# The first 24 units of a hybrid encoder layer: written order, split square sums, and a shorter dt product

## The chip, the cores and the metric

The kernel runs on one core of a Trainium2 chip. The time is device microseconds of that core for one execution. TensorE (PE; its weight loads are listed as PEld) multiplies, VectorE (DVE), ScalarE (ACT) and GpSimd (POOL) do the elementwise work, and loads are issued on the queues of SyncE (SP) and GpSimd. Products go to PSUM, from which the other engines collect them.

## The reference

The kernel computes one step of a two-layer encoder trunk on 256 prompt tokens and 64 sample tokens, 320 columns in all, with a model width of 2048. Each layer modulates a normalized input with a shift and a scale that depend on a condition vector, mixes, normalizes and adds:

```python
def modulate(x, c, w_ada, b_ada, g_pre):
    mod = jax.nn.silu(c) @ w_ada + b_ada
    shift, scale, gate = jnp.split(mod[:, None, :], 3, axis=-1)
    return rms_norm(x, g_pre) * (1 + scale) + shift, gate

# the even layer: state space heads and sliding-window attention share one input projection
z, xbc, dt_raw, q, k, v, g_att = jnp.split(h @ w_in, cuts, axis=-1)
xbc, conv_new = causal_conv(xbc, conv_prev, conv_w)
dt = jax.nn.softplus(dt_raw + dt_bias)
# ... chunked scan, attention with sinks, gates, norm ...
out = jnp.concatenate([y_ssm, y_att], axis=-1) @ w_out
```

The odd layer is a gated short convolution between two projections. All inputs and outputs are 32-bit.

## The kernel before

Features lie on the 128 partitions, tokens along the free dimension. A k-tile is 128 input features, 16 of them for the width 2048. A unit is 128 output features of a projection: 16 k-tiles, each with three products of 128x128 weights and 128x320 activations. Both operands are split into a rounded part and a rest (`wh` and `wl` of the weights, `hh` and `hl` of the activations), and the products are wh.hh, wh.hl and wl.hh (L169 to L171 in `block`). `split` makes wh on ScalarE (L149) and wl on VectorE (L150), eight weight tiles at a time.

The first layer begins while nothing is known. The input x (four tiles of four k-tiles) is squared on ScalarE and summed on VectorE in two chains over all 16 k-tiles (`sumsq`, L325 and L329); three small products, `ss0t`, sum over the partitions; `rstd` refines an inverse root on VectorE from a bit trick in three rounds and spreads it to all partitions with the products `r0b`. Meanwhile the modulation (shift and scale, one pair of numbers per feature) comes from products with `w_ada`: the first k-tile's from the first half of a small table (`ada_first`, tiles `adaf`), the second's from its other half, those of the others by blocks of 512 columns (two k-tiles, 4 MB each) in four loads of 1 MB and 16 products each (`ada_pe`, L219, tiles `adap`). The last block of the scale and shift, block 7, is multiplied on VectorE instead (`ada_side`, L250, tiles `adas` and `adac`), at a rate of 0.24 k-tiles per four entries of a product block. `modulate` makes hh and hl of a k-tile: a step on VectorE (L341), hh on ScalarE (L342), hl on VectorE (L343), each for the prompt and the sample columns apart.

Since the modulation arrives slowly, the first 24 units (k, v, and two of the four query and gate groups) go through the k-tiles in pieces: k-tile 0 for all 24 units, k-tile 1 for all, then k-tiles 2 and 3, 4 to 7, 8 to 11 and 12 to 15. After each piece the result of a unit is added from PSUM into a tile in memory (`start_unit`, L416; the first piece is copied by ScalarE, L405). The tiles of k, v, q and g are `acc`, `q` and `g`.

A scheduler sets the order of each engine's instructions, by priorities, and moves independent ones past each other; the order in the source is a start. Buffers: weights `w` in 3 buffers of 1 MB (the loads of `ada_pe` use them too), large activations in 21 buffers G, small ones in 20 buffers S, PSUM in 3 + 4 + 1 banks.

After the 24 units come attention, the other projections of the even layer with the scan, its output projection, and the odd layer. `dt` is one unit of 32 useful columns (48 products, tile `pdt`) behind the query and gate units.

Of the kernel before, what the change touches and what calls it, by code (L numbers as in the profile page):

```python
# [8 lines left out]
F32 = mybir.dt.float32  # L9
F32R = mybir.dt.float32r  # L10
# [14 lines left out]
SPE = 20  # L25
WAIT_S, WAIT_T = 6, 2
AHEAD = 3
RATE_0, RATE_A, RATE_B, RATE_C, RATE_D = 0.24, 0.55, 0.2, 0.6, 0.14
# [4 lines left out]
def hybrid_stream_step(ctx: ExitStack, tc: tile.TileContext, i, o):  # L33
    nc = tc.nc
    V, S, G, PE = nc.vector, nc.scalar, nc.gpsimd, nc.tensor
# [40 lines left out]
    for g in range(4):  # L76
        nc.sync.dma_start(xin[g], i["xT"][:, 4 * g : 4 * g + 4, :])
# [4 lines left out]
    for n in range(2):  # L82
        nc.sync.dma_start(early[n][:, 0:8, :], i["ws1"][0][n])
# [17 lines left out]
    S.activation(cs[:, :, 0:2], cT, AF.Silu)  # L101
    es = const.tile([128, 2, 32], F32, name="es")
# [5 lines left out]
    jobs, tasks, wait = [], [], [0]  # L108
# [39 lines left out]
    def split(dst_h, dst_l, src):  # L148
        S.activation(dst_h, src, AF.Copy)  # L149
        V.tensor_tensor(dst_l, src, dst_h.bitcast(F32), op=ALU.subtract)  # L150

    def block(src, name, entries, h, pool=wp):


        if early:
            w = early.pop(0)
        else:
            w = pool.tile([128, 16 if pool is wp else 8, 128], F32, tag="w" if pool is wp else "G", name=name)
            nc.sync.dma_start(w[:, 0 : len(entries), :], src)
        for hf in range(len(entries) // 8):  # L160
            wh = wp.tile([128, 8, 128], F32R, tag="wh", name=f"{name}h{hf}")
            wl = wp.tile([128, 8, 128], F32R, tag="wl", name=f"{name}l{hf}")
            split(wh, wl, w[:, 8 * hf : 8 * hf + 8, :])

            def mm(wh=wh, wl=wl, part=entries[8 * hf : 8 * hf + 8]):
                for n, (get, kt, st, en, then) in enumerate(part):
                    ps = get()
                    xh, xl = h[0][kt // 4][:, kt % 4, :], h[1][kt // 4][:, kt % 4, :]
                    PE.matmul(ps, lhsT=wh[:, n, :], rhs=xh, start=st, stop=False)  # L169
                    PE.matmul(ps, lhsT=wh[:, n, :], rhs=xl, start=False, stop=False)  # L170
                    PE.matmul(ps, lhsT=wl[:, n, :], rhs=xh, start=False, stop=en)  # L171
                    if then:
                        then(ps)
                    if n % 4 == 3:
                        yield

            jobs.append(mm)
            while len(jobs) > LOOK:
                run()
# [45 lines left out]
    def ada_side(blocks):  # L225
# [14 lines left out]
        for n, (l, b, kt) in enumerate(kts):  # L240
# [10 lines left out]
            if kt == 15:  # L251
                ps = psa.tile([128, 128], F32, tag="ada", name=f"adap{l}_{b}")
                for s in range(2):
                    for q in range(4):
                        PE.matmul(ps[32 * q : 32 * q + 32, :], lhsT=es[:, s, :],
                                  rhs=acc[s][:, 128 * q : 128 * q + 128], start=s == 0, stop=s == 1)
                ada_end(l, b, ps)
            yield 1

    def ada_end(l, b, ps, one=None):  # L260
        row = wk.tile([128, 128], F32, tag="arow", name=f"adar{l}_{b}_{one}")
        nr = 128 if one is None else 64
        S.activation(row[0:nr], ps[0:nr], AF.Copy)  # L263
        pt = sps([128, 128], f"adat{l}_{b}_{one}")
        PE.transpose(pt[:, 0:nr], row[0:nr], ident[0:nr, 0:nr])
# [24 lines left out]
    def rstd(ps, n, name, table=False):  # L290
# [6 lines left out]
        V.tensor_scalar(v, ps, 1.0 / n, EPS, op0=ALU.mult, op1=ALU.add)  # L297
        V.tensor_scalar(vh, ps, -0.5 / n, -0.5 * EPS, op0=ALU.mult, op1=ALU.add)
# [17 lines left out]
    def by_token(acc, name, one):  # L316

        ps = sps([128, 3], name)
        for b, (t0, _, _) in enumerate(TB):
            PE.matmul(ps[:, b : b + 1], lhsT=acc[:, t0 : t0 + 128], rhs=one, start=True, stop=True)  # L320
        return ps

# [29 lines left out]
    V.tensor_tensor(acc0, acc0, sums[1], op=ALU.add)
# [3 lines left out]
    del first[-4:]

    def ada_first(t):

        ps = psa.tile([128, 128], F32, tag="ada", name=f"adaf{t}")  # L360
        for kt in range(16):
            for q in range(2):
                PE.matmul(ps[32 * q : 32 * q + 32, :], lhsT=cs[:, kt, :],  # L363
                          rhs=w0[4 * t + kt // 4][:, kt % 4, 128 * q : 128 * q + 128], start=kt == 0, stop=kt == 15)
        ada_end(0, 0, ps, t)

    ada_first(0)

    ep = ev.enter_context(tc.tile_pool(name="ep", bufs=1))
# [23 lines left out]
    PIECES = ((0, 1), (1, 1), (2, 2), (4, 4), (8, 4), (12, 4))  # L393

    def start_unit(n, ps, j):
# [8 lines left out]
        if j == 0:  # L404
            S.activation(a, ps, AF.Copy)  # L405
            return
        end = j == len(PIECES) - 1
        if end and g == 0:
            for s0, s1, d0 in ((0, 256, 0), (256, 320, 384)):
                V.tensor_tensor(kT[u][:, d0 : d0 + s1 - s0], ps[:, s0:s1], a[:, s0:s1], op=ALU.add)  # L410
            G.dma_start(o["nk"][:, u, 0, :], kT[u][:, 128:256])
# [5 lines left out]
        if end and g == 1:  # L417
            for m, t0, nt in ((0, 0, 128), (1, 128, 128), (3, 256, 64)):
                pt = sps([128, 128], f"vp{u}_{m}")
                PE.transpose(pt[0:nt, :], dst[:, t0 : t0 + nt], ident)  # L420
                S.activation(vt[m][:, 128 * u : 128 * u + 128], pt[0:nt, :], AF.Copy)

    modulate(xin, rsb, 0, 0, 1, h0)
    for j, (k0, nk) in enumerate(PIECES):
        nxt = PIECES[j + 1] if j + 1 < len(PIECES) else None
        left = [2 * nxt[1] if nxt and j else 0]
        aside = j == len(PIECES) - 2
        if aside:
            left[0] -= 4
        if j == 1:  # L430
            side["gen"], side["rate"] = ada_side([(0, 7)]), RATE_0
        total = left[0]

        def then(n, ps, j=j, left=left, total=total, nxt=nxt):
            start_unit(n, ps, j)
            if j == 0 and n == 8:
                ada_first(1)
                modulate(xin, rsb, 0, 1, 1, h0)
            while left[0] and (total - left[0]) < total * (n + 1) / 19:
                ada_pe(*first.pop(0))  # L440
                left[0] -= 1
                if not left[0] and not aside:
                    modulate(xin, rsb, 0, *nxt, h0)
            if aside and n == 17:
                finish_side()
                modulate(xin, rsb, 0, *nxt, h0)

        src = i["ws1"][k0] if nk == 1 else i["ws2"] if nk == 2 else i["ws4"][k0 // 4 - 1]
        nu = 8 if nk == 1 else 16 // nk
        for g in range(24 // nu):  # L450
            en = []
            for u in range(nu):
                n = nu * g + u
                get = once(f"s{j}_{n}")
                en += [(get, k0 + k, k == 0, k == nk - 1,
                        (lambda ps, n=n, f=then: f(n, ps)) if k == nk - 1 else None) for k in range(nk)]
            block(src[g], f"ws{j}{g}", en, h0, act if j < 2 else wp)
# [205 lines left out]
    unit(wie[16], "dt", h0, steps)  # L663
# [504 lines left out]
```

## Time and profile before

| what | value |
|---|---|
| median of 3 runs (2166.16 to 2169.08) | 2168.01 us |
| the profiled execution | 2171.02 us, span of its instructions 2169.3 us |
| mean granted clock of TensorE | 0.994 |
| PE, PEld, DVE, ACT, POOL busy | 98%, 95%, 65%, 41%, 7% |
| first product of the 24 units | 24.75 us |
| last product of the 24 units | 243.3 us |
| moved in the first 216 us | 62.8 MB, 291 GB/s |

Times in a profile are us from the span's start. In a row of a group the shapes are partitions x elements, then the count, the busy time, the mean duration of one in ns, and the idle time before them with what ended it. A row of a wait names the engine that waited, the one it waited for, the total, the number of times and the longest. A product in 32-bit form leaves two records on PE, so the 16 products of one `ada_pe` show as 32.

### The profile page before, as it was taken

The numbers are of one execution on the slowest core, as the hardware profiler recorded it, in microseconds if no ns is written. First come the engines' busy times: TensorE is split into PE (matmuls) and PEld (weight loads), VectorE is DVE, ScalarE is ACT, GpSimd is POOL, SyncE is SP. The second block draws the span as 40 slices with busy tenths as digits, with TensorE's granted clock in tenths as the row PEclk, the third lists the DMA queues.
The fourth block names the chain that finished last, engine by engine and source line by source line (L and its number), as shares of the span: only waits on it lengthen the run. The fifth ranks groups of instructions, "written<-read, shape, count | busy, mean of one in ns | idle before, by whom it ended". The sixth has DMA issues, their size and how long they took to land.

```text
span 2169.3 us, 38007 instructions
## 1 busy us (share of the span) xinstructions
PE 2124.2 (98%) x15582; PEld 2056.5 (95%) x15582; DVE 1412.8 (65%) x2295; ACT 884.9 (41%) x1442; POOL 154.2 (7%) x370
## 2 busy tenths in 40 slices
PE   7999999999999999999999999999999999999997
PEld 6889999999999999997999999999999999999996
DVE  5876788897577878996755555555345554444444
ACT  5233455543465555355433333333333333333343
POOL 1000000000132223102000000000000000000001
PEclk9999999999999999999999999999999999999998
DMA  8886455466455556775554454545444454444441
GB/s 314 325 313 212 167 179 181 168 230 231 164 192 176 178 183 210 251 285 217 175 172 166 173 176 161 178 166 190 154 172 159 175 175 143 154 155 140 153 156 68
DMA packets 85758, 408.81 MB, mean 188 GB/s; under 512 B 10544, under 2 KB 11472, under 8 KB 46416
## 3 DMA queue, kind: packets, MB, share of 16 engines
q1 hardware_dynamic: 80496, 392.22, 51.8%
q0 software_dynamic: 5088, 14.16, 2.0%
q8 instruction: 122, 2.00, 0.4%
q14 instruction: 52, 0.43, 0.1%
HBM read 400.35 MB, written 5.99 MB: 187 GB/s over the span
## 4 chain that ended last, share of the span: by engine, by line
PE 90%; DVE 4%; DMA 2%; issue 1%; ACT 1%; POOL 1%; POOLq 0%; SPq 0%; DVEq 0%; ACTq 0%
PE pc L169 13%; PE pc L170 13%; PE pc L171 13%; PE px L169 3%; PE px L171 3%; PE px L170 3%; PE s L169 2%; PE s L171 2%; PE s L170 2%; PE pz L169 2%; PE pz L170 2%; PE poe L169 2%; PE pod L169 2%; PE pod L171 2%; PE poe L170 2%; PE pz L171 2%
## 5 line engine op out<-in xcount | busy, mean ns | idle before, releaser
L250 DVE SCALAR_TENSOR_TENSOR adac<-adas,cs,adac 128x512 f32<-128x512 f32 x420 | 300.2, 745 | 53.2 <-DMA adas<-in_wada 53.0
L956 POOL COPY ncc<-cp 128x2 f32<-128x2 f32 x32 | 6.0, 186 | 933.8 <-DVE cp L954 933.8
L219 PE MATMUL adap<-adaw,cs 128*32 128x128 f32 x1152 | 43.2, 284 | 3.5 <-DMA adaw<-in_wada 3.5
L219 PEld LDWEIGHTS adap<-adaw,cs 128*32 128x32 f32 x1152 | 31.6, 113 | 12.1 <-issue 6.3
L676 POOL COPY nca<-xp 128x3 f32<-128x3 f32 x24 | 22.3, 929 | 196.8 <-ACT xp L674 196.8
L961 DVE SCALAR_TENSOR_TENSOR cc<-cp,ccw,cc 128x322 f32<-128x322 f32 x64 | 35.3, 551 | 1.1
L512 ACT ACTIVATE pr<-s,mx 128x192 f32<-128x192 f32 (+2 forms) x80 | 29.8, 406 | 13.0 <-DVE mx L507 13.0
L710 ACT ACTIVATE sg<-sg,acum 128x128 f32<-128x128 f32 (+1 forms) x96 | 29.3, 376 | 12.9 <-POOL sg L702 12.9
L954 DVE TENSOR_TENSOR cp<-pc,u 128x256 f32<-128x256 f32 x31 | 13.2, 425 | 31.0 <-PE pc L171 30.8
L342 ACT ACTIVATE hh<-mt,mod 128x256 fp32r<-128x256 f32 x64 | 23.7, 419 | 20.9 <-DVE mt L341 20.7
L416 DVE TENSOR_TENSOR g<-s,g 128x320 f32<-128x320 f32 x40 | 19.0, 485 | 12.5 <-PE s L171 12.5
L681 DVE SCALAR_TENSOR_TENSOR cv<-xp,cw,cv 128x323 f32<-128x323 f32 x48 | 26.5, 552 | 0.6
L969 DVE TENSOR_TENSOR sgg<-pc,sgg 128x320 f32<-128x320 f32 x31 | 15.1, 488 | 17.4 <-PE pc L171 17.3
L879 DVE TENSOR_TENSOR oo<-poe,oo 128x320 f32<-128x320 f32 x16 | 7.9, 492 | 25.6 <-PE poe L171 25.6
L416 DVE TENSOR_TENSOR q<-s,q 128x320 f32<-128x320 f32 x40 | 18.9, 486 | 7.8 <-PE s L171 7.4
L702 POOL TENSOR_SCALAR_AFFINE_SELECT sg<-sg 128x512 f32<-128x512 f32 (+1 forms) x24 | 21.6, 911 | 30.0 <-DMA sg<-acs_b 29.9
L416 DVE TENSOR_TENSOR acc<-s,acc 128x320 f32<-128x320 f32 x32 | 15.3, 487 | 12.3 <-PE s L171 12.0
L363 PE MATMUL adaf<-w,cs 128*32 128x128 f32 x128 | 10.4, 311 | 12.8 <-ACT ss L325 12.6
L343 DVE SCALAR_TENSOR_TENSOR hl<-mt,mod,hh 128x256 fp32r<-128x256 f32 x64 | 21.5, 379 | 1.3 <-ACT hh L342 1.1
L363 PEld LDWEIGHTS adaf<-w,cs 128*32 128x32 f32 x128 | 8.1, 125 | 13.8 <-ACT ss L325 12.6
L263 ACT ACTIVATE adar_None<-adap 128x128 f32<-128x128 f32 x23 | 6.3, 273 | 34.8 <-PE adap L219 29.3
L512 ACT ACTIVATION_READ_ACCUMULATOR pr<-s,mx 128x1 f32 x80 | 17.9, 224 | 0.0
(2529 smaller groups left out, 8742.0 us busy)
## 6 DMA issues: line engine op xcount, KB each, us to landing
wc<-in_wio SPq DMA_DIRECT2D x124, 1024.0 KB, 4.9
adas<-in_wada SPq DMA_DIRECT2D x224, 256.0 KB, 5.9
adaw<-in_wada SPq DMA_DIRECT2D x36, 1024.0 KB, 7.0
wx<-in_wie SPq DMA_DIRECT2D x24, 1024.0 KB, 5.0
ws<-in_ws SPq DMA_DIRECT2D x21, 1024.0 KB, 6.9
wq<-in_wie SPq DMA_DIRECT2D x16, 1024.0 KB, 5.0
wz<-in_wie SPq DMA_DIRECT2D x16, 1024.0 KB, 4.9
woa<-in_woe SPq DMA_DIRECT2D x16, 1024.0 KB, 5.0
```

Source lines behind the costliest of these rows:

```text
L169: PE.matmul(ps, lhsT=wh[:, n, :], rhs=xh, start=st, stop=False)
L170: PE.matmul(ps, lhsT=wh[:, n, :], rhs=xl, start=False, stop=False)
L171: PE.matmul(ps, lhsT=wl[:, n, :], rhs=xh, start=False, stop=en)
L219: PE.matmul(ps[32 * q : 32 * q + 32, :], lhsT=cs[:, kt, :], rhs=(w[k] if raw else w[:, k, :])[:, 128 * q : 128 * q + 128], start=kt == 0, ...
L250: V.scalar_tensor_tensor(acc[s], w, c, acc[s], op0=ALU.mult, op1=ALU.add)
L342: S.activation(hi, t[:, a:b], AF.Identity, bias=sh)
L416: V.tensor_tensor(dst, ps, a, op=ALU.add)
L512: S.activation(pr[m][u // 2][:, u % 2, a : a + CH[c][2]], ss[m][u // 2][:, u % 2, a : a + CH[c][2]], AF.Exp, bias=mx[:, j, u : u + 1], sca ...
L676: G.tensor_copy(nca[:, ci, 0, :], xp[:, 256:259])
L681: V.scalar_tensor_tensor(cv, xp[:, n : n + 323], cw[:, ci, n : n + 1], cv, op0=ALU.mult, op1=ALU.add)
L710: S.activation(sgs[b][n][:, h, :], sgs[b][n][:, h, :], AF.Exp, bias=acum[0:nt, b, hd : hd + 1])
L961: V.scalar_tensor_tensor(cv, xp[:, m : m + 322], ccw[:, c, m : m + 1], cv, op0=ALU.mult, op1=ALU.add)
```

## The change

It touches the stretch up to the end of the 24 units, and `dt`.

- **Order.** From the squares to the end of the 24 units every instruction of TensorE and SyncE is kept in the order of the source, and so are single steps of VectorE and ScalarE (the first k-tiles' x times rs, hh, hl and weight split). Lists of delayed steps (`lag`, `todo`) and a plan by finished units say where the modulation products, their transposes and the next hh and hl stand. The modulation products come in pairs of `ada_pe`.
- **Start.** The squares of k-tiles 0 to 11 and 12 to 15 are two sums with products of their own (`ss0a`, `ss0t`); the mean of the first is added in `rstd`, which now takes ScalarE's square root and one round. x and the first weights are loaded in smaller pieces, the table of the modulation uses four column strips of PE instead of two, and three products without use (`warm`) stand in PE's order.
- **k-tiles 0 and 1.** Units 0 to 15 take k-tile 0 alone and then k-tile 1 alone; units 16 to 23 take both at once. Every third of the first copies is VectorE's.
- **Activations.** x is multiplied by rs in place on VectorE; hh is one ScalarE step from it; the rest hl is made with a ScalarE step (shift minus hh) and a VectorE step.
- **Loads.** `ada_pe` takes its weights from the buffers G in half-size tiles, up to 4 MB ahead. The small loads of GpSimd's queue (caches, biases, convolution weights) are issued only after the first k unit is written out. Block 7 runs at 0.36.
- **dt.** The 32 weight columns' rounded part and rest stand side by side in one weight tile, so that two products per k-tile do (32 in all); a small product adds the two halves up.
- The buffers S are 19 instead of 20.

```diff
-SPE = 20
+SPE = 19
-RATE_0, RATE_A, RATE_B, RATE_C, RATE_D = 0.24, 0.55, 0.2, 0.6, 0.14
+RATE_0, RATE_A, RATE_B, RATE_C, RATE_D = 0.36, 0.55, 0.2, 0.6, 0.14
+        def __getattr__(self, name):
+            f = getattr(self.eng, name)
+            def call(*a, **k):
+                ins = f(*a, **k)
+                return tc.keep_in_program_order(ins) if pin[0] else ins
+            return call
+    PE, SP = Engine(nc.tensor), Engine(nc.sync)
...
+    prev = [None, None]
+    for kt in range(12):
+        sq, m = xsq(kt, S), kt % 2
+        if kt > 1:
+            plus(sums[m], prev[m], sq)
+        prev[m] = sums[m] if kt > 1 else sq
+    plus(sums[0], sums[0], sums[1])
+    sq12, sq13, sq14, sq15 = [xsq(kt, V if kt == 15 else S) for kt in range(12, 16)]
+    plus(sums[2], sq12, sq13)
+    plus(sq14, sq14, sq15)
+    plus(sums[2], sums[2], sq14)
+    warm = mmps("warm")
+    ps0 = psa.tile([128, 128], F32, tag="ada", name="adaf0")
+    base = mean(by_token(sums[0], "ss0a", ones[:, 0:1]), D, "r0m")
+    ada_first(0, range(8), ps0)
+    ss = by_token(sums[2], "ss0t", ones[:, 0:1])
+    ada_first(0, range(8, 16), ps0)
+    row0 = ada_row(0, 0, ps0, 0)
+    idle(1, 128)
+    ada_turn(0, 0, row0, 0)
+    rsp = rstd(ss, D, "r0", True, base)
+    idle(2, 320)
...
+    def known(kts, step, turn=None):
+        got = {}
+        if turn:
+            lag(step, *turn)
+        lag(2 * step, lambda: got.update({kts[0]: shifted(kts[0])}))
+        lag(3 * step, lambda: got.update({kts[1]: shifted(kts[1])}))
+        lag(3 * step, lambda: rest(kts[0], got[kts[0]]))
+        lag(4 * step, lambda: rest(kts[1], got[kts[1]]))
+
+    def ada_pair(depth, step):
+        for _ in range(2):
+            (l, b, sub), raw = fetched.pop(0)
+            ada_pe(l, b, sub, raw=raw, end=False)
+        ada_fetch(depth)
...
+    plan = {1: [lambda: tc.keep_in_program_order(S.activation(rsb, rsp, AF.Copy))], 2: [lambda: normal(1, rsb)],
+            6: [lambda: later_first(range(8))], 10: [lambda: later_first(range(8, 16))],
+            24: [lambda: ada_pair(2, 2)], 32: [lambda: ada_pair(4, 2)]}
...
+    for k0, nk, at, lead in ((2, 2, (3, 8, 13, 18), 4), (4, 4, (2, 7, 12, 17), 3), (8, 4, (4, 12), 3), (12, 4, (), 0)):
+        base = 40 + 24 * (0, 1, 2, 3)[(2, 4, 8, 12).index(k0)]
+        plan = {base + c: [lambda lead=lead: ada_pair(lead, 1)] for c in at}
...
+                    for m in range(2):
+                        PE.matmul(ps[0:96], lhsT=wh[:, n, 0:96], rhs=h[m][kt // 4][:, kt % 4, :],
+                                  start=kt == 0 and m == 0, stop=kt == 15 and m == 1)
```

What moved, at three places. First, TensorE at the start. Before (`adaf` is the modulation table, `ss0t` and `r0b` belong to the inverse root):

```order
L363 MATMUL adaf_218<-w_0_91,cs 32x128 x3
L320 MATMUL ss0t<-ones,ss_136 128x1 x3
L363 MATMUL adaf_218<-w_0_91,cs 32x128 x5
L363 MATMUL adaf_218<-w_1_92,cs 32x128 x7
L313 MATMUL r0b<-r0d,ones 128x128 x2
L313 MATMUL r0b<-r0d,ones 128x64
L363 MATMUL adaf_218<-w_1_92,cs 32x128
L363 MATMUL adaf_218<-w_2_93,cs 32x128 x8
L363 MATMUL adaf_218<-w_3_94,cs 32x128 x8
L265 MATMUL adat_0_0_253<-ident,adar_0_0_251 128x64
```

and with the change:

```order
L47 MATMUL ss0a<-ones,ss_145 128x1 x3
L47 MATMUL adaf_195<-w_0_92,cs 32x128 x8
L47 MATMUL adaf_195<-w_1_93,cs 32x128 x8
L47 MATMUL ss0t<-ones,ss_147 128x1 x3
L47 MATMUL adaf_195<-w_2_94,cs 32x128 x8
L47 MATMUL adaf_195<-w_3_95,cs 32x128 x8
L47 MATMUL warm<-x_83,ones 128x128
L47 MATMUL adat_0_0_241<-fold,adar_0_0_238 128x64
L47 MATMUL r0b<-r0d,ones 128x128 x2
L47 MATMUL r0b<-r0d,ones 128x64
L47 MATMUL warm<-x_83,ones 128x320 x2
```

The whole first half of the table and its transpose now stand ahead of `r0b`, and 16 of its products ahead of `ss0t`.

Second, VectorE where k-tiles 2 and 3 are made ready. Before (`mod` is the modulation, g the sums of gate units, `mt` and `hl` the steps L341 and L343):

```order
L276 TENSOR_TENSOR mod_134<-mod_134,gpre 128x4
L416 TENSOR_TENSOR g_295<-s_21_723,g_295 128x320
L341 SCALAR_TENSOR_TENSOR mt_2_669<-x_83,mod_134,rsb 128x256
L341 SCALAR_TENSOR_TENSOR mt_2_669<-x_83,mod_134,rsb 128x64
L341 SCALAR_TENSOR_TENSOR mt_3_676<-x_83,mod_134,rsb 128x256
L341 SCALAR_TENSOR_TENSOR mt_3_676<-x_83,mod_134,rsb 128x64
L416 TENSOR_TENSOR g_295<-s_22_728,g_295 128x320
L343 SCALAR_TENSOR_TENSOR hl_0_297<-mt_2_669,mod_134,hh_0_296 128x256
L343 SCALAR_TENSOR_TENSOR hl_0_297<-mt_2_669,mod_134,hh_0_296 128x64
```

and with the change (sc are the units of k-tile 1, ws_0l the weight rests of k-tiles 2 and 3):

```order
L317 TENSOR_TENSOR mod_141<-adat_1_None,bada 128x2x4
L591 TENSOR_TENSOR q_286<-sc_10_693,q_286 128x5x64
L319 TENSOR_TENSOR mod_141<-mod_141,gpre 128x4
L591 TENSOR_TENSOR q_286<-sc_11_698,q_286 128x5x64
L174 TENSOR_TENSOR ws_0l_580<-ws_0_577,ws_0h_579 128x1024
L174 TENSOR_TENSOR ws_0l_676<-ws_0_577,ws_0h_675 128x1024
L591 TENSOR_TENSOR g_288<-sc_12_708,g_288 128x320
L591 TENSOR_TENSOR g_288<-sc_13_713,g_288 128x320
L486 SCALAR_TENSOR_TENSOR hl_0_293<-x_83,mod_141,mt_2_703 128x256
L486 SCALAR_TENSOR_TENSOR hl_0_293<-x_83,mod_141,mt_2_703 128x64
```

Between the modulation and hl of k-tile 2 there now stand both weight splits of the block that uses it.

Third, the SP queue at k-tiles 2 and 3. Before (ws are weights of units, adaw the modulation's, adas those of block 7):

```order
L159 DMA ws_895<-in_ws 128x2048
L215 DMA adaw_3_0_918<-in_wada 128x2048
L215 DMA adaw_3_1_952<-in_wada 128x2048
L234 DMA adas_7_5_990<-in_wada 128x512
L215 DMA adaw_3_2_1002<-in_wada 128x2048
L159 DMA ws_1028<-in_ws 128x2048
```

and with the change:

```order
L47 DMA ws_1_737<-in_ws 128x2048
L47 DMA adaw_00_804<-in_wada 128x1024
L47 DMA adaw_01_805<-in_wada 128x1024
L47 DMA adaw_10_808<-in_wada 128x1024
L47 DMA adaw_11_809<-in_wada 128x1024
L47 DMA adaw_20_886<-in_wada 128x1024
L47 DMA adaw_21_887<-in_wada 128x1024
L47 DMA adaw_30_890<-in_wada 128x1024
L47 DMA adaw_31_891<-in_wada 128x1024
L47 DMA ws_2_896<-in_ws 128x2048
```

A whole block of the modulation, 4 MB, stands between two weight blocks, in eight loads.

More of the change, by code (lines that the diff above doesn't have):

```diff
@@ L321, in by_token, with mean @@
         return ps
+    def mean(ps, n, name):
+        b = wk.tile([128, 3], F32, tag="rb", name=name)
+        V.tensor_scalar(b, ps, 1.0 / n, EPS, op0=ALU.mult, op1=ALU.add)
+        return b
     def sumsq(acc, t, first, name):
@@ L356, in hybrid_stream_step @@
[L356 to L369, printed above, removed]
+    pin[0] = True
+    S.activation(wk.tile([128, 1], F32, tag="rt", name="table"), cs[:, 0, 0:1], AF.Sqrt, scale=0.0)
@@ new lines, in idle @@
+    def idle(n, m):
+        for _ in range(n):
+            PE.matmul(warm[:, 0:m], lhsT=ones, rhs=xin[0][:, 0, 0:m], start=True, stop=True)
+    warm = mmps("warm")
[8 more added lines that the diff above has]
+    rsp = rstd(ss, D, "r0", True, base)
@@ L403, in start_unit @@
             a = dst = gps[g // 2 - 1][:, u, :]
-        if j == 0:
-            S.activation(a, ps, AF.Copy)
+        if n not in begun:
+            begun.add(n)
+            if n < 16 and n % 3 == 2:
+                last["V"] = V.tensor_copy(a, ps)
+            else:
+                last["S"] = S.activation(a, ps, AF.Copy)
             return
-        end = j == len(PIECES) - 1
         if end and g == 0:
@@ L417, in start_unit @@
         if end and g == 1:
[L418 to L449, printed above, removed]
-        for g in range(24 // nu):
[L451 to L457, printed above, removed]
@@ new lines, in then, with products @@
+    def then(n, ps, end, plan):
+        start_unit(n, ps, end)
+        seen[0] += 1
+        now = [t for t in todo if t[0] <= 1]
+        for t in todo:
+            t[0] -= 1
+        todo[:] = [t for t in todo if t[0] > 0]
+        for _, f, a in now:
+            f(*a)
+        for f in plan.get(seen[0], ()):
+            f()
+    def products(src, name, units, kts, plan, end=False, **how):
+        by_kt = isinstance(src, list)
+        get = {n: once(f"s{name}_{n}", bank) for n in units}
+        en = [(get[n], k, k == kts[0], k == kts[-1],
+               (lambda ps, n=n: then(n, ps, end, plan)) if k == kts[-1] else None)
+              for n, k in ([(n, k) for k in kts for n in units] if by_kt else [(n, k) for n in units for k in kts])]
+        block(src, "ws" + name, en, h0, wp, **how)
@@ new lines, in hybrid_stream_step, with side_end, side7, end7 @@
+    look[0] = LOOK
+    ada_fetch(2)
+    products(w1[1][0], "c0", range(8), [1], plan)
+    ada_fetch(4)
+    products(w1[1][1], "c1", range(8, 16), [1], plan)
+    def side_end(l, b, ps):
+        row = ada_row(l, b, ps)
+        lag(1, ada_turn, l, b, row)
+    def side7():
+        side["gen"], side["rate"] = ada_side([(0, 7)], side_end), RATE_0
+    def end7():
+        finish_side()
+        for n, kt in enumerate((14, 15)):
+            lag(n, normal, kt, rsb)
+        known((14, 15), 1)
@@ L459, in hybrid_stream_step @@
+    flush()
+    while todo:
+        todo.pop(0)[1]()
+    pin[0] = False
     side["gen"] = ada_side([(0, b) for b in range(8, 12)] + [(1, b) for b in range(5)])
```

260 lines of the change are left out of this document (210 added, 50 removed).

## The prediction

> **What bounds the kernel now.** I read the page first: how busy the engines are, and where.
>
> ```profile
> span 2169.3 us, 38007 instructions
> PE 2124.2 (98%) x15582; PEld 2056.5 (95%) x15582; DVE 1412.8 (65%) x2295; ACT 884.9 (41%) x1442; POOL 154.2 (7%) x370
> PE   7999999999999999999999999999999999999997
> ```
>
> TensorE sets the end. A busy PE can still be paced below its best, so I set elapsed time against products. A clean block of 48 products is the yardstick, then the six stretches of the first 24 units: start, k-tiles 0 and 1, 2 and 3, 4 to 7, 8 to 11, 12 to 15.
>
> ```profile
> 480.52:487.56 7.04, 7.04 (x50) 7.04 (x49) 0.42 (x1) 1.00 0.51 173
> ...
> 0.00:26.70 26.70, 11.79 (x107) 9.27 (x107) 14.78 (x48) 10.94 (x24) 10.16 (x24) 1.00 0.94 341
> 26.70:59.46 32.76, 30.34 (x310) 26.55 (x310) 20.14 (x42) 18.76 (x38) 0.00 (x0) 1.00 0.79 302
> 59.46:91.66 32.20, 32.04 (x369) 27.95 (x370) 26.31 (x54) 7.44 (x12) 0.00 (x0) 0.95 0.88 325
> 91.66:148.71 57.05, 54.63 (x582) 49.87 (x581) 41.21 (x77) 16.94 (x27) 0.00 (x0) 1.00 0.88 316
> 148.71:199.12 50.41, 48.18 (x436) 46.08 (x435) 37.58 (x68) 15.71 (x22) 0.00 (x0) 1.00 0.68 237
> 199.12:243.12 44.00, 44.00 (x302) 43.39 (x301) 29.95 (x48) 16.39 (x25) 5.42 (x10) 1.00 0.57 189
> ```
>
> The columns are the stretch, its length, and busy time of PE, PEld, DVE, ACT and POOL, then granted clock, DMA share and GB/s (the first row has no DVE and POOL). One product costs 7.04/48 = 0.147 us. The chain of waits gives the price of the modulation products (32 records, four k-tiles of one 512-column block):
>
> ```profile
> 51.62 1.01 PE adap L219 x32
> 52.63 0.34 PE s L171
> ```
>
> 1.01 us, and the product behind them comes 0.19 late (0.34 after the one before it, for 0.15), so 1.2 us a group. With 4, 7, 9, 4 and 0 such groups in the five product stretches, and the products of each (141, 144, then 288 three times), the clean times are: 20.7 + 4.8 + 2.5 for the rest of the first table = 28.0; 21.1 + 8.4 = 29.5; 42.2 + 10.8 = 53.0; 42.2 + 4.8 + 0.8 for the side block = 47.8; 44.0. Against the rows the kernel loses 4.8, 2.7, 4.0, 2.6 and 0: **14 us**, beside a start of 26.7 us. Who is waited for:
>
> ```profile
> PE s L169 <- ACT hh L342: 3.1, 2, 1.6
> PE adap L219 <- DMA adaw<-in_wada: 2.4, 3, 1.5
> PE s L170 <- DVE hl L343: 1.2, 1, 1.2
> PE s L169 <- DVE g L416: 0.8, 1, 0.8
> PE s L171 <- DVE ws30l L150: 0.5, 1, 0.5
> ```
>
> The waits for hh and hl are at the boundaries between groups of k-tiles, where the order on VectorE and ScalarE put weight splits ahead of the next activations.
>
> **The start, step by step.** The old chain:
>
> ```profile
> 2.66 8.39 DMA x<-in_xT
> ...
> 12.79 0.49 DVE ss L329
> 13.30 0.50 DVE ss L352
> 13.85 1.45 PE ss0t L320 x6
> ...
> 18.10 1.54 PE r0b L313 x6
> 19.65 2.22 PE adaf L363 x34
> 21.89 0.27 ACT adar L263
> ...
> 26.05 0.60 DVE hl L343 x2
> 26.70 0.41 PE s L170
> ```
>
> and, of the timeline, the rest of the old table's first half:
>
> ```profile
> 15.22 2.77 PE L363 MATMUL adaf<-w,cs 128*32 128x128 f32 x24
> ```
>
> Now x still lands near 11 us. The first chain of squares (k-tiles 0 to 11) ends near 11.8, since two adds (0.49 and 0.50 in the rows) follow the last of its squares; ss0a takes the 1.45 of ss0t, to 13.3. The 16 modulation products that now stand between ss0a and ss0t cost about 1.9 at this clock (the row has 24 records in 2.77 us, in two column strips; 32 records in four strips take half of what 32 took, 3.7), so ss0t runs from 15.2 to 16.65, no earlier than now. Behind it the square root replaces two of three refinement rounds:
>
> ```profile
> 989.71 0.83 PE L320 MATMUL rp0t<-ones,facc 128*128 128x1 f32 x6 [0.18 <-DVE facc L329]
> ...
> 992.15 0.88 PE L313 MATMUL rp0b<-rp0d,ones 128*128 128x128 f32 x6
> ```
>
> 990.54 to 992.15 is 1.6 us there, where the start has 2.8 (15.3 to 18.1): 1.2 saved. But PE has the second half of the table first: 1.9, the copy 0.27 and the transpose, to 19.2; then r0b, 1.2 (between the 0.88 and 1.54 above), to 20.4. Then x times rs (0.48, the L416 rows), half a weight split (0.6) and hl (0.76, from the L343 rows of 479 and 278 ns): the first unbroken product at about **22.2**. The old one is 26.70 less three products already done, 26.3. **Gain 4.1**, at best 5.5 (PE never delaying ss0t), at worst 2.5. The extra idle products run while PE waits anyway; the two late ones lie under the 1.8 us of x, split and hl on VectorE.
>
> **Between the k-tiles.** Groups come in pairs: 12 switches of 0.19 less, 2.3. The table's second half costs 2.0 (two halves at 1.01). For the stalls I walked the order at the one place where VectorE is short: k-tile 1 for 16 units.
>
> ```profile
> L416 DVE TENSOR_TENSOR acc<-s,acc 128x320 f32<-128x320 f32 x32 | 15.3, 487 | 12.3 <-PE s L171 12.0
> L343 DVE SCALAR_TENSOR_TENSOR hl<-mt,mod,hh 128x256 fp32r<-128x256 f32 x16 | 7.7, 479 | 1.3 <-ACT hh L342 1.1
> L343 DVE SCALAR_TENSOR_TENSOR hl<-mt,mod,hh 128x64 fp32r<-128x64 f32 x16 | 4.4, 278 | 0.0
> L150 DVE TENSOR_TENSOR ws20l<-ws,ws20h 128x1024 fp32r<-128x1024 f32 x2 | 2.4, 1216 | 0.0
> L250 DVE SCALAR_TENSOR_TENSOR adac<-adas,cs,adac 128x512 f32<-128x512 f32 x36 | 25.7, 743 | 1.9 <-DMA adas<-in_wada 1.9
> ```
>
> A unit of three products takes 0.44 on PE, its add 0.48 on VectorE. Eight adds, two normalizing steps and a split: 10 x 0.48 + 1.22 = 6.0 against 3.5 + 2.1 (pair) on PE, a stall of 0.6. The next eight units take PE 3.5; VectorE has, up to hl of k-tile 2, six adds 2.9, two mod steps 0.3, two splits 2.4 and hl 0.76 = 6.4, and starts level: PE waits **3.3 us** for hl. Behind it hl of k-tile 3 comes 1.7 later, just when it is wanted. So this stretch is 21.1 + 2.0 + 4.0 + 1.0 (five switches) + 3.9 = 32.0, to 54.2.
>
> Such a wait has a second price; the row of the wait, and the clock behind it:
>
> ```profile
> 59.46 0.56 PE L169 MATMUL s<-hh,ws20h 128*128 128x320 f32 x2 [1.63 <-ACT hh L342]
> 61.00:64.00 3.00, 3.00 (x34) 0.50 0.83 340
> 60.00:65.00 5.00, 5.00 (x45) 0.66 0.71 253
> ```
>
> After the 1.63 us wait the granted clock was half, and over the five us of the last row 0.66: 5 x 0.34 = 1.7 us lost. A longer wait should do it again, so I take 1.7 in the new stretch too. The Trainium skill, "TensorE: Matmul & The Clock Gate", section "The HAM clock gate", says that the clock falls after at least one idle window of about 3.4 us; by that rule a 3.3 us wait would hardly do it and the sum would end 1.7 lower. Here 1.63 us sufficed, so the trace decides for the price.
>
> **Loads.** SP now holds the weights of units behind the modulation loads, and these wait for the products that free their buffers.
>
> ```profile
> 30.00:40.00 10.00, 10.00 (x88) 8.96 (x87) 4.04 (x8) 8.98 (x21) 0.00 (x0) 1.00 1.02 417
> 60.00:70.00 10.00, 10.00 (x103) 8.14 (x103) 7.78 (x15) 1.10 (x2) 0.00 (x0) 0.83 0.77 270
> ```
>
> K-tiles 2 and 3 need 3 MB of weights, 8 MB of modulation and 1 MB for the side block in 30 us: 400 GB/s, against 417 seen. K-tiles 4 to 7 need 6 + 8 + 2.2 in 51 us: 318. A weight block that is issued at the start of a pair, with 1 to 2 MB ahead of it, lands some 9 us later (2 us, and 3 MB at 417 GB/s) and is usable 2.3 after that (a split on ScalarE, one on VectorE); the walk finds it 0 to 0.6 late. I take 0.5, 1.0 and 0.3 in the three stretches (bounds: 0, and 8 in all). VectorE: 11.5 for adds, 14.7 for splits, 5.4 for the next k-tiles, 13 for the side block at 0.36 (8.7 k-tiles of two steps), so 45 of 51 us: it fits, with little slack.
>
> So: 21.1 + 8.1 + 0.8 + 0.5 + 1.7 = 32.2, to 86.4; 42.2 + 8.1 + 0.9 + 1.0 = 52.2, to 138.6; 42.2 + 4.0 + 1.2 + 0.3 = 47.7, to 186.3; 44.0, to 230.3. The old end is 243.1: **12.8 gained**.
>
> **dt.** 32 products for 48, on a PE with nothing else in between:
>
> ```profile
> L169 PE MATMUL pdt<-hh,wdth x16: 308/309/412, 396.5 to 403.2; 128*128 128x320 f32 x16
> ```
>
> 16 x 0.147 = **2.35**. If ScalarE's attention work is late there, down to 1. One S buffer less (19) costs nothing I can see: writers into those tiles already wait for PE, not for a buffer. Unknown, taken as 0; bounds: 2 lost (a third of a microsecond, as the hl and ws30l waits, at six attention steps), 1 gained. The later stretches are PE-bound (a 9 in nearly every slice), so what is gained stays.
>
> Sum: 12.8 + 2.35 = 15 us. The profiled execution took 2171.0 (span 2169.3), so it would take 2156; the median is 3 lower, 2168.0, so **2153**.
>
> **Rivals.**
> 1. Forecast, 2153: chance 0.60 (2148 to 2158).
> 2. Loads late, 2161: the row of k-tiles 2 and 3 moved 325 GB/s, not 417. At 325, 12 MB take 37 us, 7 more than PE needs: gain 8. For it: SP's written order lets a weight block wait behind modulation loads. Against: smaller loads, up to 4 MB fetched ahead. 0.16. The Trainium skill, "DMA: Bandwidth & Descriptors", "Specifications", puts a core's share of HBM at 358 GB/s, which would make it 33.5 us, 3.5 more; the row at 417 says otherwise.
> 3. Better, 2146: ss0t not held up (1.4), the hl wait hidden by finished products' banks (3), full clock (1.7). 0.12.
> 4. Slower, 2178: with TensorE in written order a late modulation load stops all products behind it, and nothing fills in. If the rate falls to the 270 GB/s that 60 to 70 us showed, k-tiles 2 to 7 (28 MB) need 104 us, 22 over the 82 planned, and 3 us more as waits halve the clock; it outweighs the gain below about 290 GB/s. Against: 302 to 325 in every loaded stretch. 0.06.
> 5. No change, 2167: the gain is given back in attention, where VectorE is busiest and now starts with the same side work. Against: PE's full slices. 0.06.
>
> 0.2% (4.3 us) is what a measurement of this kernel can tell. **Faster 0.86, same 0.08, slower 0.06.** Range 2145 to 2162: it holds cases 1 and 3, and most of 2.
>
> **What would show it.** First unbroken product near 22 (24 or more: the table on PE cost more); a PE wait of 2 to 4 us for hl near 50, with half the clock behind it; k-tile 4 beginning near 86, the stage ending near 230; no wait for adaw above 1 us; 32 dt products in 4.7 us. Wrong if waits for ws splits appear in every pair, or if attention's stretches grow by what the stage gave.

## The result, and the profile after

The changed kernel takes 2181.28 us (median of 4 runs, 2180.41 to 2185.22) against 2168.16 us of the kernel before on the same chip: a ratio of 1.0065, with a 95% interval of 1.0053 to 1.0077. It is slower by 13 us, where 15 less were forecast. The profiled execution took 2180.94 us. From its page, the span and the busy times:

```profile
span 2179.2 us, 38042 instructions
PE 2120.8 (97%) x15583; PEld 2058.1 (94%) x15583; DVE 1408.9 (65%) x2275; ACT 895.3 (41%) x1469; POOL 156.2 (7%) x371
```

TensorE has about the same work (2124.2 before), in a span that is 9.9 us longer: waiting, not working. The stretches of the first 24 units, cut where the products of the next k-tiles begin to run (same columns as in the table of before):

```profile
0.00:24.40 24.40, 10.25 (x92) 8.37 (x92) 11.98 (x43) 11.35 (x26) 2.71 (x10) 1.00 0.91 348
24.40:56.05 31.65, 28.71 (x339) 26.43 (x339) 20.47 (x41) 19.06 (x39) 0.00 (x0) 1.00 0.95 359
56.05:89.90 33.85, 30.04 (x401) 27.91 (x401) 19.93 (x46) 11.09 (x22) 0.00 (x0) 1.00 0.93 342
89.90:149.90 60.00, 54.28 (x547) 51.57 (x548) 43.13 (x75) 19.73 (x33) 0.00 (x0) 0.94 0.81 291
149.90:201.20 51.30, 49.08 (x435) 47.62 (x435) 38.85 (x65) 19.53 (x31) 0.00 (x0) 0.97 0.51 189
201.20:248.10 46.90, 44.38 (x302) 43.39 (x301) 26.16 (x41) 17.45 (x26) 12.88 (x25) 1.00 0.53 172
```

The two granted clocks under 1.00 are new in these places. What TensorE waited for between 24.4 and 248 us, the longest totals (the total in us, how often, the longest):

```profile
PE s L47 <- DVE ws_2l L174: 3.3, 1, 3.3
PE s L47 <- DVE ws_0l L174: 3.1, 2, 2.2
PE s L47 <- ACT ws_4h L170: 2.8, 1, 2.8
PE s L47 <- DVE hl L486: 2.8, 2, 2.4
PE vp L47 <- DVE vT L591: 2.5, 4, 0.7
PE s L47 <- DVE ws_4l L174: 1.6, 1, 1.6
```

Four of the six are weight splits (11.3 us with a smaller one of 0.5); e1 below shows that the loads in front of them were late. No wait for a modulation load (adaw) shows. Behind the 24 units there is a second loss. I took the start of every weight block of TensorE in both traces and subtracted:

| first product of | before, us | after minus before, us |
|---|---|---|
| last of the 24 units (its last product) | 242.98 | +5.01 |
| dt | 396.54 | +3.80 |
| z unit 0, behind dt | 403.68 | +1.43 |
| z unit 1 | 416.23 | +3.66 |
| wos1, in the output projection of the scan | 858.60 | +3.33 |
| wos2 | 868.72 | +9.63 |
| end | 2169.31 | +9.92 |

So three things are to be explained: 5.0 us lost in the 24 units where 12.8 were to be won; dt's 2.37 won and 2.23 given back in the block behind it; and 6.3 us lost between wos1 and wos2, some 600 us behind the 24 units and 460 behind `dt`. Of the last, the waits of TensorE from 840 to 900 us, before (first fence) and after (second):

```profile
PE adat_None L265 <- ACT adar_None L263: 1.0, 1, 1.0
```

```profile
PE adat_None L47 <- ACT adar_None L300: 3.2, 1, 3.2
PE adap L47 <- DVE adac L285: 1.2, 1, 1.2
```

The modulation's own chain (`adac` on VectorE, product, row copied by ScalarE, transpose) stopped TensorE there, and the clock was halved for 6.8 us behind it.

### The profile page after: what moved, and what is told of

It reads as the page before. It is cut to its first block, busy times and chain, and to the rows that moved or that the text cites. A ratio compares the mean times of both kernels' runs of the same rounds, so it can differ in the third digit from the quotient of the medians.

```text
span 2179.2 us, 38042 instructions
## 1 busy us (share of the span) xinstructions
PE 2120.8 (97%) x15583; PEld 2058.1 (94%) x15583; DVE 1408.9 (65%) x2275; ACT 895.3 (41%) x1469; POOL 156.2 (7%) x371
## 3 DMA queue, kind: packets, MB, share of 16 engines
q1 hardware_dynamic: 84528, 392.22, 51.3%
## 4 chain that ended last, share of the span: by engine, by line
PE 93%; DVE 2%; DMA 1%; ACT 1%; issue 1%; POOL 0%; SPq 0%; POOLq 0%; DVEq 0%; ACTq 0%
PE pc L47 40%; PE px L47 8%; PE s L47 6%; PE pq L47 5%; PE poe L47 5%; PE pod L47 5%; PE pz L47 5%; PE poa L47 5%; PE pot L47 2%; PE pos L47 2%; PE adap L47 2%; PE c L47 1%; PE o L47 1%; PE pt L47 1%; PE st L47 1%
## 5 line engine op out<-in xcount | busy, mean ns | idle before, releaser
L47 PE MATMUL adap<-adaw,cs 128*32 128x128 f32 x1152 | 37.6, 275 | 1.7 <-DMA adaw<-in_wada 1.7
L1237 DVE TENSOR_TENSOR sgg<-pc,sgg 128x320 f32<-128x320 f32 x31 | 15.2, 490 | 19.9 <-PE pc L47 19.6
L949 DVE SCALAR_TENSOR_TENSOR cv<-xp,convaw,cv 128x323 f32<-128x323 f32 x48 | 26.5, 552 | 0.5
L47 PE MATMUL s<-hh,ws_0l 128*128 128x320 f32 x64 | 20.6, 322 | 3.1 <-DVE ws_0l L174 3.1
L47 PE MATMUL s<-hl,ws_0h 128*128 128x320 f32 x64 | 20.6, 322 | 2.8 <-DVE hl L486 2.8
L47 PE MATMUL s<-hh,ws_2l 128*128 128x320 f32 x64 | 19.9, 311 | 3.3 <-DVE ws_2l L174 3.3
L47 PE MATMUL s<-hh,ws_0h 128*128 128x320 f32 x64 | 20.8, 326 | 0.5 <-ACT ws_0h L170 0.5
L47 PE MATMUL s<-hh,ws_1h 128*128 128x320 f32 x64 | 20.5, 321 | 0.0
L47 PE MATMUL s<-hh,ws_2h 128*128 128x320 f32 x64 | 20.1, 314 | 0.0
L47 PE MATMUL s<-hh,ws_1l 128*128 128x320 f32 x64 | 19.8, 309 | 0.0
```

The source lines that it names most:

```text
L47: ins = f(*a, **k)
L949: V.scalar_tensor_tensor(cv, xp[:, n : n + 323], cw[:, ci, n : n + 1], cv, op0=ALU.mult, op1=ALU.add)
L1237: V.tensor_tensor(sg, ps, sg, op=ALU.mult)
```

## The experiments

Each is the kernel before or the changed one with one or a few edits. Times are medians, and a ratio compares a kernel with the kernel before as measured beside it, whose median was 2166.9 to 2168.2 us; "less than the change" is counted from 2181.28. Places in the program are compared by trace. One execution's stage can differ by some 3 us from another's with the same code (the 24 units of the changed kernel ended 5.0 us after those of before in one trace and 2.0 in another, e3, whose stage is the same), so smaller differences there prove nothing.

**e1: weight blocks one block earlier.**

```diff
+    coming = [w1[1][0], w1[1][1]] + [i["ws2"][g] for g in range(3)] + [i["ws4"][p][g] for p in range(3) for g in range(6)]
+    def load_ahead(depth):
+        while coming and len(early) < depth:
+            src = coming.pop(0)
+            w = wp.tile([128, 16, 128], F32, tag="w", name="wsn")
+            SP.dma_start(w[:, 0 : src.shape[1], :], src)
+            early.append(w)
...
         for g in range(24 // nu):
+            load_ahead(2)
             products(src[g], f"{k0}_{g}", range(nu * g, nu * g + nu), list(range(k0, k0 + nk)), plan, k0 == 12,
```

`block` takes its weights from `early` as long as there are any, so each block finds a load that was issued one block before.

> The changed kernel, but each weight block of the first 24 units is loaded one block earlier (the order of SP alone changes; the bytes are the same). Theory 1, order of loads: the blocks are late because their loads stand behind modulation loads that wait for TensorE's own products; then TensorE's waits for ws splits (12 us) shrink to under 4, the stage ends near 240 instead of 248, and the time is 2170 to 2175 instead of 2181. Rival, rate of memory (DMA was 0.93 busy between 53 and 86 us): the waits move from ws to adaw and the time stays within 3 us of 2181. Rival, VectorE late with the splits: waits for ws splits stay as they are, 2181.

2176.01 us, ratio 1.0042 (1.0027 to 1.0057), 5 less than the change. The waits of its 24 units:

```profile
PE s L47 <- DVE hl L486: 4.0, 3, 2.0
PE vp L47 <- DVE vT L591: 2.5, 4, 0.7
PE sc L47 <- DVE acc L591: 1.5, 3, 0.6
PE s L47 <- ACT hh L472: 1.3, 1, 1.3
PE s L47 <- DVE ws_0l L174: 0.5, 1, 0.5
```

Waits for weight splits fall from 11 us to 0.5 with the same bytes, so neither the rate of memory nor VectorE's splits made them late: their place in the queue did. The stage ended 0.5 us before the old one, 5.5 better than in the trace of the change (2.5 better than in e3's), not 12: with the products in fixed order the next waits (hl, hh, acc, vT) come up behind, and the clock was half for 13.7 us of the stage where the change had 10.2.

**e2: TensorE's order left to the scheduler.**

```diff
-    PE, SP = Engine(nc.tensor), Engine(nc.sync)
+    PE, SP = nc.tensor, Engine(nc.sync)
```

> The changed kernel with TensorE's order left to the scheduler (SP in written order as before). Theory 1: the weight blocks are issued at the same places, so they stay late and most of the 12 us remain; the scheduler can fill in a modulation group or the finished half of a block, worth 2 to 5 us: 2176 to 2180. Rival, TensorE's written order is itself what costs: the waits for ws go below 4 us and the time comes to 2170 or less. If the scheduler's guesses are worse than the written order: 2183 or more.

2170.22 us, ratio 1.0011 (1.0001 to 1.0020): 11 less than the change, more than twice the most I expected and near the rival, and the stage ends 6.1 us before the old one. The expectation held that the same late loads would stay late. But the waits for weight splits halve, to 5.3 us, and the queue of SP shows why. First the changed kernel, then e2 (start, time from the start of the first issue to the end of the last, and how many):

```profile
121.55 0.52 SPq L47 DMA_DIRECT2D ws<-in_ws  x1
122.17 16.57 SPq L47 DMA_DIRECT2D adaw<-in_wada  x4
...
139.32 0.43 SPq L47 DMA_DIRECT2D ws<-in_ws  x1
```

```profile
121.73 0.75 SPq L47 DMA_DIRECT2D ws<-in_ws  x1
122.58 6.60 SPq L47 DMA_DIRECT2D adaw<-in_wada  x4
...
130.74 0.33 SPq L47 DMA_DIRECT2D ws<-in_ws  x1
```

A modulation load needs a buffer that TensorE's modulation products free. In the changed kernel SP waited for them from 122 to 137 us: TensorE stood in front of a late weight block (ws_4, 4.4 us), then ran it at half the clock, and the next modulation products stood behind that block's first products in the written order. In e2 TensorE ran such products while it waited:

```profile
128.16 1.07 PE L254 MATMUL adap<-adaw,cs 128*32 128x128 f32 x30
129.62 0.33 PE L306 MATMUL adat_None<-ident,adar_None 128*128 128x128 f32 x1 [0.39 <-ACT adar_None L300]
129.89 1.08 PE L254 MATMUL adap<-adaw,cs 128*32 128x128 f32 x32
131.20 0.41 PE L204 MATMUL s<-hh,ws_4h 128*128 128x320 f32 x1 [0.23 <-ACT ws_4h L170]
```

That frees the buffers, and SP goes on. What the memory moved, the changed kernel from 120 to 140 us and e2 from 110 to 140 us (last number, GB/s):

```profile
120.00:130.00 10.00, 7.08 (x47) 6.56 (x45) 4.55 (x10) 1.79 (x2) 0.00 (x0) 0.99 1.00 345
130.00:140.00 10.00, 8.52 (x92) 8.05 (x93) 6.74 (x11) 2.31 (x4) 0.00 (x0) 0.67 0.38 145
```

```profile
110.00:120.00 10.00, 10.00 (x139) 9.41 (x140) 8.52 (x17) 3.42 (x6) 0.00 (x0) 1.00 0.27 98
120.00:130.00 10.00, 9.61 (x103) 8.44 (x95) 4.69 (x10) 0.28 (x1) 0.00 (x0) 1.00 1.00 334
130.00:140.00 10.00, 9.67 (x89) 9.14 (x88) 9.62 (x16) 7.05 (x12) 0.00 (x0) 1.00 1.02 417
```

So the loss feeds itself: a late block stops TensorE, TensorE stops SP, the memory falls to 145 GB/s, and the load of a weight block behind is issued at 139.3 instead of 130.7 us; TensorE waited 2.2 us for a split of that block too, up to 152.5. The idle memory alone is not the loss: in e2 SP waited 13.1 us for modulation products as well, and only 98 GB/s were moved from 110 to 120 us, but TensorE had products to run and waited 0.23 us for the block behind. One such turn is shown here; how much of the 11 us came from the chain and how much from each block's own place is not separated.

**e12: SP's order left to the scheduler, TensorE's kept.**

```diff
-    PE, SP = Engine(nc.tensor), Engine(nc.sync)
+    PE, SP = Engine(nc.tensor), nc.sync
```

> The changed kernel with SP's order left to the scheduler and TensorE in written order. The scheduler puts the loads of the stage in nearly the same order as the source has them (two weight blocks of k-tile 1 move ahead of the first modulation loads, and one more block ahead of three modulation loads near 120 us). Theory: what makes the blocks late is the place of their loads in the source together with a TensorE that may not run the waiting modulation products early; keeping SP in written order adds nothing: 2179 to 2183. Rival, SP's written order is the cause: 2170 to 2174.

2179.65 us, ratio 1.0059 (1.0042 to 1.0076): as the change. Keeping SP in program order adds nothing. The scheduler put the loads in nearly the same order, so this run does not test another place of the weight loads; e1 does, and there the place counts.

**e3 and e8: the count of the side work.** The modulation work on VectorE (`ada_side`) advances by a count at every half block of products. The kernel before starts that count with two half blocks of the stage still unrun (four ticks of 0.55, 2.2 k-tiles); the change runs them first (its `flush()`), so that all later modulation work stands two k-tiles later in the program. e3 corrects that in the changed kernel with the line below; e8 puts the delay into the kernel before, with -1.92 in the same line:

```diff
+    side["due"] = 2.32
     side["rate"] = RATE_A
```

> The changed kernel, but the count of the modulation work on VectorE starts at 2.32 instead of 0.28 behind the 24 units, so that it is as far in the program as in the kernel before (there four ticks of 0.55 fell behind this point, that the change does ahead of it). Theory: the 6 us lost between 868 and 878 us come from this: the copy of the modulation row stands two k-tiles later, behind exponentials on ScalarE that wait for GpSimd; then that stretch takes what it took before and the time is 2175 to 2178. Rival, the loss there belongs to the clock or to the loads and falls anywhere: 2180 to 2183, with the stretch from wos1 to wos2 still near 16 us instead of 10.

> The kernel before, with only the count of the modulation work set 2.04 lower behind the 24 units, which is where the change leaves it. Theory: the loss between wos1 and wos2 appears here too, with nothing else changed: 5 to 7.5 us, 2173 to 2176. Rival, it needs the changed stage: 2168 within 2.

e3: 2177.73 us, ratio 1.0045 (1.0030 to 1.0061); from wos1 to wos2 it takes what the kernel before takes, within 0.02 us, and the 6.3 are gone. Its four runs lie between 2171.83 and 2179.66, and the trace is of the fastest, so the median of 3.6 us less says little on the size; e8 is the better measure. e8: 2174.79 us, ratio 1.0032 (1.0021 to 1.0043); the same stretch grows by 6.8 us. Its waits there:

```profile
PE adat_None L265 <- ACT adar_None L263: 4.8, 1, 4.8
PE adap L255 <- DVE adac L250: 1.0, 1, 1.0
```

So this loss needs none of the new order in the 24 units, only the count that they leave behind. ScalarE shows the mechanism, first in the kernel before, then in the changed one:

```profile
860.29 0.27 ACT L263 ACTIVATE adar_None<-adap 128x128 f32<-128x128 f32 x1
860.45 1.86 ACT L710 ACTIVATE sg<-sg,acum 128x128 f32<-128x128 f32 x6
```

```profile
872.64 0.40 ACT L978 ACTIVATE sg<-sg,acum 128x128 f32<-128x128 f32 x1 [0.59 <-POOL sg L970]
872.95 1.04 ACT L170 ACTIVATE wos2h<-wos 128x1024 fp32r<-128x1024 f32 x1
873.90 1.56 ACT L978 ACTIVATE sg<-sg,acum 128x128 f32<-128x128 f32 x5
875.36 0.26 ACT L300 ACTIVATE adar_None<-adap 128x128 f32<-128x128 f32 x1
```

The copy `adar` now stands behind six exponentials (sg), the first of which waits 0.59 us for GpSimd, and a weight split between them; before, it stood ahead of six. TensorE's transpose waits 3.2 us for it, and half the clock behind that wait adds to the loss.

**e4 and e10: the short dt alone, and the split behind it.** e4 is the kernel before with the new dt (and 19 small buffers: the small matrix that adds the halves up takes the place of the twentieth). e10 adds:

```diff
-            split(wh, wl, w[:, 8 * hf : 8 * hf + 8, :])
+            if name == "wz00" and hf:
+                V.tensor_copy(wh, w[:, 8:16, :])
+                V.tensor_tensor(wl, w[:, 8:16, :], wh.bitcast(F32), op=ALU.subtract)
+            else:
+                split(wh, wl, w[:, 8 * hf : 8 * hf + 8, :])
```

> The kernel before with only the new dt (32 products, and 19 instead of 20 small buffers, since the small matrix of its sum takes the place). Theory: the 2.35 us are off the path and stay off: 2165.5 to 2166. Rival, given back in attention, as the alignment of the two traces suggests (2.2 us lost in the first z block): 2168 within 1 us; then the wait stands before the z unit that follows the last attention step.

> As e4 (the kernel before with the short dt alone), with the same split on VectorE. Theory: 1 to 2.4 us less than e4's loss, so 2164.5 to 2166 and a first z block that is 1 us or more shorter than e4's 15.1. Rival, attention's chain: as e4, 2166.5 to 2168.

e4: 2166.52 us, ratio 1.0001 (0.9992 to 1.0010): no gain, as the rival had it. By trace dt takes 2.37 us less and the z block behind it 2.59 more. The wait, and then ScalarE's row for that block's second split in the kernel before and in e4:

```profile
PE pz L169 <- ACT wz00h L149: 1.6, 1, 1.6
```

```profile
405.07 1.12 ACT L149 ACTIVATE wz00h<-wz 128x1024 fp32r<-128x1024 f32 x1
```

```profile
405.12 1.11 ACT L149 ACTIVATE wz00h<-wz 128x1024 fp32r<-128x1024 f32 x1
```

The split runs at the same time however short dt is, since it stands behind the exponentials of attention's last step. With it on VectorE (e10) the z block gives back 1.1 instead of 2.6, which shows the place; the time (2166.86, ratio 0.9999, 0.9990 to 1.0008) is the rival's, and cannot resolve so little. The rest is open: TensorE then waits 0.8 us in attention's transposes (pt).

**e5 and e6: both cures.** e5 is e2 with e3's line; e6 adds e1's loads.

> The changed kernel with both single corrections: TensorE's order left to the scheduler, and the modulation count set to 2.32 behind the 24 units. If the two losses are separate they add: the stage ends near 237 (6 us before the kernel before), about 1.6 more by the wos blocks, and nothing is lost between wos1 and wos2: 2161 to 2163 (ratio near 0.997). Rival, the loss at wos1 depends on when the stage ends and not on the count alone: 2168 to 2171.

> As e5, and the weight blocks one block earlier as in e1. Theory: the waits for ws that remained with a free TensorE (5 us in the stage) go as well: 2157 to 2160. Rival, the two are cures for one and the same thing, and what e1 showed next (waits for hl and acc on VectorE) takes over: 2161 to 2164.

e5: 2161.34 us, ratio 0.9971 (0.9959 to 0.9982), inside the forecast. In its trace the stage ends 6.1 us before the old one, as in e2, and nothing is lost between wos1 and wos2, as in e3: the two losses are separate. (By medians e2 gains 11.1, e3 3.6 and both together 19.9; e3's figure is the uncertain one.) e6: 2164.30 us, 0.9987 (0.9978 to 0.9995): no further gain, but 3 us more than e5, and 4.0 us of waits for ws_0 stay in its stage. With TensorE free the earlier loads bring nothing; that both cure one and the same thing fits this, but is not shown, and where the 3 us go is open.

**e7: TensorE in written order, mended.** e1's loads, e3's line, and:

```diff
-            lag(1, turn)
+            lag(3, turn)
...
-            PE.matmul(warm[:, 0:m], lhsT=ones, rhs=xin[0][:, 0, 0:m], start=True, stop=True)
+            PE.matmul(warm[:, 0:m], lhsT=ones, rhs=xin[1][:, 0, 0:m], start=True, stop=True)
```

> TensorE in written order as in the change, with four corrections: weight blocks one block earlier, the modulation count at 2.32, the transposes of v three units later instead of one, and the idle products reading another tile of x than the one that the next step overwrites. Theory on the start: the step of x on VectorE waits for the two idle products because they read x; without that the second product of the units starts 1.1 us earlier, at 23.2 to 23.4 instead of 24.4. The waits for vT (2.5 us) go. Stage end 237 to 240, time 2162 to 2166. Rival, the written order of TensorE cannot be mended by loads and single steps: stage end over 242, 2168 or more.

2161.40 us, ratio 0.9971 (0.9960 to 0.9982), as e5 and 0.6 under the forecast. So a written order can be as good as the free one, with four corrections together, of which two can be told apart in the trace: the vT waits go, and the start is earlier. The chain that set the start, in the changed kernel and in e7 (start, time, what):

```profile
19.87 1.05 PE r0b L47 x6
20.92 1.15 PE warm L47 x4
...
22.09 0.50 DVE x L459
```

```profile
19.97 1.29 PE r0b L47 x6
...
21.29 0.50 DVE x L459
```

The two idle products read the very tile that the next step overwrites, so VectorE waited 1.15 us for work without use. In e7 it starts 0.80 earlier (r0b itself ended 0.34 later), and the second product of the units at 23.57 instead of 24.38.

**e9 and e11: e5 and e7 with e10's split on VectorE.**

> As e5, and the second half of the first z unit's weights (the block behind dt) is split on VectorE instead of ScalarE. Theory: the gain of dt is given back because that split stands behind the twelve exponentials of the last attention step on ScalarE, which end at the same time whether dt is long or short; VectorE has room there (3 of 7 us busy), so the wait of 1.2 us goes and 1 to 2.4 us are kept: the first z block 12.6 us again instead of 14.8, time 2159 to 2160.5. Rival, the attention chain itself (transposes and values behind the exponentials) holds TensorE: the wait moves behind the split, time as e5, 2161.3.

> As e7 (TensorE in written order, with the four corrections), with the same split on VectorE. Theory: 1 to 2.4 us under e7's 2161.4, so 2159 to 2160.4. Rival: 2161.4.

e9: 2161.53 us, ratio 0.9970 (0.9959 to 0.9981); e11: 2161.02 us, 0.9966 (0.9953 to 0.9978). In both traces the z block gives back 0.8 instead of 2.3, but the times are those of e5 and e7 within their spread: the rivals were right, and where the 1.5 us go is not shown. e5, e7, e9 and e11 are faster than the kernel before by 0.3%.

## Why the prediction was wrong

| step | forecast, us | measured, us |
|---|---|---|
| first unbroken product | 22.2 | 24.4 |
| k-tiles 0 and 1 | 32.0 | 31.7 |
| k-tiles 2 and 3 | 32.2 | 33.9 |
| k-tiles 4 to 7 | 52.2 | 60.0 |
| k-tiles 8 to 11 | 47.7 | 51.3 |
| k-tiles 12 to 15 | 44.0 | 46.9 |
| dt, with the block behind it | -2.35 | -0.1 |
| everything else behind the 24 units | 0 | +5.0 |

**The start** missed by 2.2. Up to r0b the working was 0.5 early (20.4 for 20.92). Then failed the sentence that the two late idle products lie under VectorE's 1.8 us: they read x, so VectorE waited for them, worth 0.8 to 1.15 (e7). The rest is the chain of x, split and hl, 2.3 for 1.84.

**K-tiles 0 and 1** came out right, with the wait for hl near 53 (2.4 for 3.3) and a stall of 0.6 before it. In the working itself the terms give 0.4 and 2.9 for the two, not 0.6 and 3.3, so that 0.6 of the 32.0 was a slip (and rival 3's terms add to 6.1, which is 2147). The half clock that I put behind the wait did not come.

**Loads: the mis-sized term, and the step that decided.** I took 0.5, 1.0 and 0.3 us of late loads (8 as the most in all) and measured 11 us of waits for weight splits; waits for ws were the sign that I had named for being wrong. I had seen that weight blocks stand behind modulation loads that wait for products, and costed only the bytes ahead of them. What was missing is that in written order TensorE's wait delays the freeing of buffers, which delays the next loads (e2); the cost of a late block is not its own lateness alone. The clock's part was also short: it was half for 6.8 and 3.4 us, in which TensorE was busy for 8.6, so that 4.3 us were lost where 1.7 was put.

**Rival 4** had the right sign and half the mechanism: a late load stops all products and nothing fills in. But it had modulation loads late, where weight blocks were, and hung this on the rate of memory, below 290 GB/s. The rate was not the limit (e1, e2: the same bytes, and 417 GB/s in e2 where the change moved 145); 145 is what the stall left over. Its chance of 0.06 was too low, since it was judged by the rate and not by the order.

**K-tiles 12 to 15** lost 2.9: the transposes of v, one unit behind VectorE's sum in written order, cost 2.5. The working has no term for them.

**dt** saves 2.37 us as worked out, but the loss I allowed for only if attention were late ("down to 1") was nearly the whole of it: 2.23 given back, since a weight split of the next block stands behind attention's exponentials (e4).

**"What is gained stays"** was the second failure, 6.3 us. A PE row of nines said that no other engine was the bound; it did not say that the order behind depends on a count, which the change shifted by two k-tiles (e8: about 7 us from that shift alone). Rival 5 looked for a give-back in attention; there it was dt's 2.2, and three times as much at wos1.

With TensorE's fixed order and the shift of the count taken away (e5) the time is 2161.3, 8 above the forecast: the 24 units gain 6.1 instead of 12.8, and dt's 2.4 are still given back (2.3); small gains behind make up a part.

## What to carry to other kernels

Before fixing an engine's order by hand, ask at each wait what that engine could do meanwhile and who waits for that work: where products free the buffers of the queue that feeds them, a fixed order can turn one late load into a chain of late loads. Side work that is spread by a count has a phase, the place in the program where each of its steps falls; a flush or a different count of steps moves it everywhere behind, and the first thing to compare is the place of its copies on the in-order engines. And filler work must not read what the next step writes.

## What the runs showed of the hardware

The granted clock of TensorE falls in windows of 3.41 us that lie on one grid through the whole execution (in the changed kernel it is half from 129.78 for 6.83 us, from 153.67 for 3.41 and from 873.88 for 6.83), and goes mostly by how busy TensorE was in the window before. Windows of the changed kernel on that grid (PE's busy time stands behind the length, the clock third from the end):

```profile
75.20:78.60 3.40, 1.70 (x11) 1.43 (x10) 2.85 (x9) 2.01 (x2) 0.00 (x0) 1.00 0.94 320
78.60:82.00 3.40, 1.80 (x12) 1.80 (x13) 2.68 (x4) 0.00 (x0) 0.00 (x0) 1.00 1.01 364
126.40:129.80 3.40, 0.60 (x3) 0.30 (x2) 0.91 (x3) 1.59 (x2) 0.00 (x0) 1.00 1.02 376
129.80:133.20 3.40, 1.79 (x7) 1.72 (x7) 3.40 (x5) 0.96 (x2) 0.00 (x0) 0.50 0.76 312
133.20:136.60 3.40, 3.40 (x14) 3.32 (x13) 1.35 (x3) 0.52 (x1) 0.00 (x0) 0.50 0.00 1
```

The wait of 3.3 us at 77 us lay over two windows, each half busy, and cost no clock; the 4.4 us in two pieces at 126 to 131 us left one window 0.18 busy, and the clock was half for two windows. In the kernel before 1.63 us sufficed, since other gaps lay in the same window:

```profile
57.40:60.80 3.40, 1.77 (x11) 1.32 (x9) 3.27 (x12) 2.33 (x5) 0.00 (x0) 1.00 0.96 317
```

Over the 14 traces (14 us to 2100 us, full clock) all 24 windows in which TensorE was busy up to 0.47 were followed by half the clock, and 9 of the 21 between 0.48 and 0.57; what decides among those 21 stays open. Six windows with more (0.60 to 0.80) were followed by it too, all between 878 and 894 us; what is special there stays open as well. So a clock loss could not be forecast by the length of a wait, as I did: the longer wait cost none and the shorter one did, and where a wait lies against the grid, and what other gaps share its window, was not known beforehand. The Trainium skill, "TensorE: Matmul & The Clock Gate", section "The HAM clock gate", gives a window of 3413 ns that runs freely, and at least one idle window as what lowers the clock. These traces bear out the first; for the second, a window that was half busy was often enough here.
